# Third convolution channel split between VectorE and GpSimd, and a head's exact scores placed ahead of a later head's first scores

## The chip, the cores and the metric

The kernel runs on one core of a Trainium2 chip. The metric is the device time of one execution in microseconds (us), as the median over the timed runs. One more execution is recorded by the hardware profiler; its own time and its span (first to last instruction) are given with the profile. TensorE is called PE in the profile, VectorE DVE, ScalarE ACT, GpSimd POOL; SP issues most of the transfers.

## The reference, cut to what matters

Two layers of an encoder block on one sequence of 512 positions with 1024 features, float32. Each layer is a half-weighted gated feed-forward block, a mixing block, a second feed-forward block and a final norm. The change lies in the mixing block, which has eight attention heads and a convolution side by side:

```python
def conv_group(u_raw, conv_w, conv_b, ln_g, ln_b):
    a, g = u_raw[..., :CONV_W], u_raw[..., CONV_W:]
    u = a * jax.nn.sigmoid(g)
    y = lax.conv_general_dilated(          # causal, depthwise, 31 taps, 512 features
        u, conv_w[:, None, :].astype(u.dtype),
        window_strides=(1,), padding=[(CONV_K - 1, 0)],
        dimension_numbers=('NWC', 'WIO', 'NWC'), feature_group_count=CONV_W)
    y = y + conv_b
    return jax.nn.silu(layer_norm(y, ln_g, ln_b))

# in each layer
attn = mla_group(...)                      # 8 heads, block-causal softmax attention
conv = conv_group(p[..., o_cv:], ...)
x = x + jnp.concatenate([attn, conv], axis=-1) @ w_out[l]
```

The layer norm of the convolution needs the sum over all 512 features at each position, so it cannot begin before all of them are convolved.

## The kernel before, in words

Features lie on the 128 partitions and the 512 positions along a row, so the 512 convolved features are four tiles of 128 x 512, which the program calls channels 0 to 3. Full-precision products are made of three passes of float32r matmuls (lines 155 to 157). Between the two feed-forward blocks of a layer stands `mix_body`: projections, the queries and keys, then the heads, the convolution, the norm of the convolution and the output projection.

**Convolution** (lines 882 to 901). The string `CONV = "DAAD"` says for each channel who works. Kind D: ScalarE writes the 31st tap and the bias into the one PSUM bank named `cv` (line 886), VectorE adds the other thirty taps one by one, each a SCALAR_TENSOR_TENSOR in that bank (line 890), and ScalarE copies the bank back to SBUF (line 900). Kind A: ScalarE writes the first term to a tile `y` in SBUF, and for each of the thirty taps ScalarE makes a product `pr` (line 894, three buffers) and GpSimd adds it to `y` (line 898). Each tap of shift s works on a row of 512 - s, so the forms run from 511 down to 482 and the width tells which tap a row is. Lines 912 to 914 add the four channels on GpSimd into `ysum` (t in the rows), and line 916 is the matmul of that sum, the first step of the norm; matmuls of the output projection whose inputs are there already stand behind it on PE.

**Channels and their inputs.** `glu` (lines 616 to 624) makes the input `u` of a channel out of two projections. Channel 2 is projected just ahead of the heads, channel 3 in the middle of the first two heads.

**Heads.** `ORDER = "t0m1s3v4o5"` with `for step in range(H + 6)` writes the program's order: in each step come t (`turn`) for head `step`, m (`maxima`) for the head one behind, s (`scores`) for the head three behind, v (`values`) four behind and o (`turn_out`) five behind. `turn` transposes queries and keys on PE (line 808), ScalarE copies them out (line 811), GpSimd casts them (line 815). `maxima` makes first scores with the cast tiles in four matmuls (line 824), VectorE takes the row maxima (line 825, four reductions), transposes them (line 827, tile `mt`), and SP's queue writes them into a row of the queries by four small transfers (line 830). `scores` makes the exact scores with that row in four matmuls (line 837) and ScalarE takes the exponentials (line 840). `values` follows (line 848).

**What sets the order.** Tile's scheduler turns the program's order into one in-order queue for each engine, after a timeline of its own; a PSUM bank (seven of the name `ps`, one `cv`) is handed on when its readers are done, which makes waits of its own. So the order in which stages are written decides which bank waits for whom.

Of the kernel before, what the change touches and what calls it, by code (L numbers as in the profile page):

```python
# [7 lines left out]
FP = mybir.dt.float32  # L8
# [3 lines left out]
AF = mybir.ActivationFunctionType  # L12
ALU = mybir.AluOpType
AX = mybir.AxisListType

P = 128
D = 1024
S = 512
# [13 lines left out]
CK = 31  # L32
# [7 lines left out]
FRB = 9  # L40
RING = 40
WIDE = 5
CONV = "DAAD"
PAUSE = 16
LATE = ((), (), (), (0, 1, 2, 3), (4, 5, 6, 7))
SEQ = "q0 R c1 q1 q2 qo k kt tt uq uk c2"
# [7 lines left out]
E3 = 3  # L54
WOG = 3
WOP = 4
ORDER = "t0m1s3v4o5"
TURN = "AA"

VECS = [("g1", 8), ("gm", 8), ("g2", 8), ("gp", 8), ("gql", 3), ("gkl", 2),  # L60
# [12 lines left out]
def encoder_kernel(ctx: ExitStack, tc: tile.TileContext, xT, consts, vecs, rgain, wgu1, wd1,  # L73
# [10 lines left out]
    psum = ctx.enter_context(tc.tile_pool(name="psum", bufs=7, space=PSUM))  # L84
    uid = [0]

    def nm(s):
        uid[0] += 1
        return f"{s}{uid[0]}"
# [4 lines left out]
    def tmp(w=S, dt=FP):  # L94
        return tmps.tile([P, w], dt, tag="t", name=nm("t"))
# [7 lines left out]
    V, A, G, T = nc.vector, nc.scalar, nc.gpsimd, nc.tensor  # L103
# [100 lines left out]
    def spread(r):  # L204

        dg = tmp()
        V.tensor_tensor(dg.rearrange("p (t j) -> p t j", t=NT),
                        ident[:, None, :].to_broadcast([P, NT, P]),
                        r[:, :, None].to_broadcast([P, NT, P]), ALU.mult)
        ps = bank()  # L210
        T.matmul(ps, ones, dg, start=True, stop=True)
        return ps
# [22 lines left out]
    order = {}  # L235
# [372 lines left out]
    def mix(l, gx, norm, done):  # L608
        with tc.tile_pool(name="k", bufs=4) as kpool:
            mix_body(kpool, l, gx, norm, done)  # L610

    def mix_body(kpool, l, gx, norm, done):
        u = []
        ys = [None if kind == "D" else kpool.tile([P, S], FP, tag="y", name=nm("y"), bufs=2) for kind in CONV]

# [251 lines left out]

        STAGES = [({"t": turn, "m": maxima, "s": scores, "v": values, "o": turn_out}[c], int(d)) for c, d in zip(ORDER[::2], ORDER[1::2])]
        for step in range(H + 6):
# [11 lines left out]
        cw, cb = vv(l, "cw"), vv(l, "cb")  # L881
        for c in range(4):
            kind = CONV[c]
            acc = psum.tile([P, S], FP, tag="cv", name=nm("cv"), bufs=1) if kind == "D" else ys[c]
            tap = lambda k: cw[:, c * CK + k:c * CK + k + 1]
            A.activation(acc, u[c], AF.Identity, scale=tap(CK - 1), bias=cb[:, c:c + 1])  # L886
            for k in range(CK - 2, -1, -1):
                s = CK - 1 - k
                if kind == "D":
                    V.scalar_tensor_tensor(acc[:, s:], u[c][:, :S - s], tap(k), acc[:, s:], ALU.mult, ALU.add)  # L890
                    continue
                pr = kpool.tile([P, S], FP, tag="pr", name=nm("pr"), bufs=3)
                if kind == "A":
                    A.activation(pr[:, s:], u[c][:, :S - s], AF.Copy, scale=tap(k))  # L894
                else:
                    G.tensor_scalar(pr[:, s:], u[c][:, :S - s], tap(k), None, ALU.mult)
                with tc.issue_after(order["keys"]) if s >= PAUSE or c > 1 else nullcontext():
                    order["conv"] = G.tensor_tensor(acc[:, s:], acc[:, s:], pr[:, s:], ALU.add).ins  # L898
            if kind == "D":
                A.copy(u[c], acc)  # L900
                ys[c] = u[c]
# [24 lines left out]
        pr = spread(r)  # L926
        early_groups(range(E3, WOG))
        lg, lb = vv(l, "lg"), vv(l, "lb")
        cv = []
        for c in range(4):  # L930
            z = tmp()
            V.tensor_tensor(z, ys[c], pr, ALU.mult)
            s = tmp()
# [224 lines left out]
```

## Time and profile before

| | |
|---|---|
| median of 3 runs (lowest, highest) | 1810.32 us (1808.76, 1815.42) |
| profiled execution: its time, its span | 1808.44 us, 1806.6 us |
| mean granted TensorE clock | 0.983 |
| PE busy | 1746.0 us (97%) |
| DVE busy | 1382.6 us (77%) |
| ACT busy | 942.3 us (52%) |
| POOL busy | 289.7 us (16%) |

A row of the timeline reads: start in us from the span's start, length in us, engine, line of the program, operation, tile written<-tiles read, count, and in brackets the idle time just before with what ended it. Rows of equal instructions that follow each other are merged. A row of a window reads: the stretch, its length, then busy time and count for PE, PE's weight loads, DVE, ACT and POOL, the granted TensorE clock (1.00 is full), the share of the DMA engines and GB/s.

### The profile page before, as it was taken

What the parts mean: (1) busy time and instruction counts of PE and PEld (TensorE: products, weight loads), DVE (VectorE), ACT (ScalarE), POOL (GpSimd) and SP (SyncE); (2) the same over time, 40 slices, a digit from 0 to 9 for tenths busy, and PEclk for the clock granted to TensorE, in tenths of its full rate; (3) what the DMA queues carried; (4) which work ended last, traced back from release to release, by engine and by line L of the source; (5) the groups of instructions that cost most, each with busy time, mean ns of one, the idle gap of its engine ahead of it and who ended that gap; (6) DMA issues with size and microseconds to landing.
All of it is one profiled execution on the core that took longest, in us unless ns stands there. A gap on an engine that the chain in (4) does not pass through costs nothing.

```text
span 1806.6 us, 22073 instructions
## 1 busy us (share of the span) xinstructions
PE 1746.0 (97%) x8006; PEld 1446.8 (80%) x8006; DVE 1382.6 (77%) x2001; ACT 942.3 (52%) x1404; POOL 289.7 (16%) x268
## 2 busy tenths in 40 slices
PE   8999999999959999999999999999999699999998
PEld 7888888888748888888888888888977488888886
DVE  8967886688828877878799778865976398688784
ACT  6534444467745544445555344454767455444453
POOL 2000000057752000000000000000687420000000
PEclk9999999999979999999999999999999799999999
DMA  9454435325106344352924344343260253544345
GB/s 288 144 171 140 150 96 151 105 77 139 26 25 209 126 155 141 107 163 81 290 94 168 112 152 143 116 134 100 74 152 2 104 129 126 177 141 126 131 123 157
DMA packets 122429, 236.74 MB, mean 131 GB/s; under 512 B 11216, under 2 KB 58832, under 8 KB 122320
## 3 DMA queue, kind: packets, MB, share of 16 engines
q1 hardware_dynamic: 118000, 222.11, 38.3%
q0 software_dynamic: 3456, 12.58, 3.8%
q8 instruction: 63, 1.03, 0.2%
q10 hardware_dynamic: 864, 0.64, 0.1%
q14 instruction: 46, 0.38, 0.1%
HBM read 207.99 MB, written 25.17 MB: 129 GB/s over the span
## 4 chain that ended last, share of the span: by engine, by line
PE 81%; POOL 6%; DVE 5%; issue 3%; ACT 2%; DMA 2%; SPq 0%; POOLq 0%; ACTq 0%; DVEq 0%
PE ps L155 26%; PE ps L157 26%; PE ps L156 26%; POOL y L898 4%; DVE cv L890 1%; DVE wl L242 1%; PE ps L837 1%; PE ps L848 1%; DMA raw<-in_wgu 1%; DVE fr L339 1%; ACT pr L894 1%; PE ps L193 0%; DMA rg<-in_rgain 0%; DMA x<-in_xT 0%; PE ps L824 0%
## 5 line engine op out<-in xcount | busy, mean ns | idle before, releaser
L156 PE MATMUL ps<-wl,r 128*128 128x512 f32 (+2 forms) x1434 | 547.9, 384 | 1.4 <-DVE wl L242 1.4
L157 PE MATMUL ps<-wh,r 128*128 128x512 f32 (+2 forms) x1434 | 545.2, 384 | 0.0
L155 PE MATMUL ps<-wh,r 128*128 128x512 f32 (+2 forms) x1434 | 529.3, 384 | 2.7 <-ACT wh L240 1.7
L240 ACT CAST wh<-fr 128x1024 fp32r<-128x1024 f32 x255 | 267.0, 1050 | 241.8 <-PE ps L157 111.3
L157 PE MATMUL ps<-r,wl 128*128 128x512 f32 x944 | 367.0, 390 | 0.5 <-POOL wl L150 0.5
L156 PE MATMUL ps<-r,wh 128*128 128x512 f32 x944 | 366.9, 390 | 0.0
L155 PE MATMUL ps<-r,wh 128*128 128x512 f32 x944 | 364.0, 395 | 0.7 <-ACT wh L144 0.5
L242 DVE TENSOR_TENSOR wl<-fr,wh 128x1024 fp32r<-128x1024 f32 x255 | 309.8, 1218 | 49.4 <-ACT wh L240 48.0
L155 PEld LDWEIGHTS ps<-wh,r 128*128 128x128 f32 x1434 | 269.4, 188 | 55.1 <-ACT wh L240 2.6
L156 PEld LDWEIGHTS ps<-wl,r 128*128 128x128 f32 x1434 | 269.6, 188 | 53.7 <-DVE wl L242 1.9
L157 PEld LDWEIGHTS ps<-wh,r 128*128 128x128 f32 x1434 | 269.4, 188 | 52.5 <-DVE r L268 0.4
L144 ACT CAST wh<-raw 128x1024 fp32r<-128x1024 f32 (+2 forms) x142 | 139.8, 990 | 217.3 <-PE ps L156 91.9
L155 PEld LDWEIGHTS ps<-r,wh 128*128 128x128 f32 x944 | 177.8, 189 | 40.6 <-ACT r L161 1.1
L156 PEld LDWEIGHTS ps<-r,wh 128*128 128x128 f32 x944 | 177.9, 188 | 38.7 <-issue 2.0
L157 PEld LDWEIGHTS ps<-r,wl 128*128 128x128 f32 x944 | 177.8, 188 | 38.7 <-POOL wl L150 1.3
L150 DVE TENSOR_TENSOR wl<-raw,wh 128x1024 fp32r<-128x1024 f32 (+3 forms) x126 | 145.8, 1159 | 76.2 <-ACT wh L144 75.4
L898 POOL TENSOR_TENSOR y<-y,pr 128x509 f32<-128x509 f32 (+15 forms) x120 | 158.2, 1319 | 48.8 <-ACT pr L894 42.7
L339 DVE TENSOR_TENSOR fr<-fr,fr 128x1024 f32<-128x1024 f32 x112 | 136.3, 1217 | 11.0 <-DMA fr<-in_wgu 11.0
L487 DVE TENSOR_TENSOR x<-ps,x 128x512 f32<-128x512 f32 x120 | 81.6, 686 | 53.8 <-PE ps L157 53.4
L369 ACT ACTIVATE e<-e,rtok 128x256 f32<-128x256 f32 x120 | 60.0, 508 | 71.6 <-DVE e L360 70.9
L894 ACT ACTIVATE pr<-r,vec 128x511 f32<-128x511 f32 (+14 forms) x120 | 82.9, 713 | 21.5 <-POOL y L898 21.5
L890 DVE SCALAR_TENSOR_TENSOR cv<-r,vec,cv 128x511 f32<-128x511 f32 (+14 forms) x120 | 88.0, 733 | 5.9 <-ACT cv L886 3.8
(199 smaller groups left out, 1630.8 us busy)
## 6 DMA issues: line engine op xcount, KB each, us to landing
fr<-in_wgu SPq DMA_DIRECT2D x175, 512.0 KB
raw<-in_wd SPq DMA_DIRECT2D x56, 512.0 KB
d<-e SPq DMA_DIRECT2D x176, 128.0 KB
r<-d SPq DMA_DIRECT2D x88, 256.0 KB
raw<-in_wd SPq DMA_DIRECT2D x32, 384.0 KB
raw<-in_wcv SPq DMA_DIRECT2D x16, 512.0 KB
raw<-in_wout SPq DMA_DIRECT2D x16, 512.0 KB
raw<-in_wgu SPq DMA_DIRECT2D x8, 512.0 KB
```

Of the source, the lines that this page charges most:

```text
L144: A.copy(hi[:, :w], raw[:, :w])
L150: (G if kind in POOLW.split() else V).tensor_tensor(lo[:, :w], raw[:, :w], hi[:, :w].bitcast(FP), ALU.subtract)
L155: T.matmul(o, lh, rh, start=first, stop=False, skip_group_check=free)
L156: T.matmul(o, lh, rl, start=False, stop=False, skip_group_check=free)
L157: T.matmul(o, ll, rh, start=False, stop=last, skip_group_check=free)
L240: order["cast"] = A.copy(hi[:, :w], src[:, :w]).ins
L242: V.tensor_tensor(lo[:, :w], src[:, :w], hi[:, :w].bitcast(FP), ALU.subtract)
L339: V.tensor_tensor(oh, ah, bh, ALU.add)
L487: V.tensor_tensor(xm, pd.rearrange("p (a t j) -> p t a j", a=4, t=NT), xm, ALU.add)
L890: V.scalar_tensor_tensor(acc[:, s:], u[c][:, :S - s], tap(k), acc[:, s:], ALU.mult, ALU.add)
L894: A.activation(pr[:, s:], u[c][:, :S - s], AF.Copy, scale=tap(k))
L898: order["conv"] = G.tensor_tensor(acc[:, s:], acc[:, s:], pr[:, s:], ALU.add).ins
```

## The change

Channel 2 becomes a new kind, M: ScalarE writes the first term into the `cv` bank, VectorE adds the taps of shift 1 to 12 there, ScalarE copies the bank to `y`, and the taps of shift 13 to 30 stay as they were (product by ScalarE, addition by GpSimd). GpSimd's own products, which no channel used, go. In the heads' order, s3 now stands ahead of m1: in each step the exact scores of the head three behind come ahead of the first scores of the head one behind. Behind `mix_body`'s norm every engine has the order it had; both layers change alike. The lines of the program behind line 43 move by one.

```diff
--- before.py
+++ after.py
@@ -40,7 +40,8 @@
 FRB = 9
 RING = 40
 WIDE = 5
-CONV = "DAAD"
+CONV = "DAMD"
+MIXED = 12
 PAUSE = 16
 LATE = ((), (), (), (0, 1, 2, 3), (4, 5, 6, 7))
 SEQ = "q0 R c1 q1 q2 qo k kt tt uq uk c2"
@@ -54,7 +55,7 @@
 E3 = 3
 WOG = 3
 WOP = 4
-ORDER = "t0m1s3v4o5"
+ORDER = "t0s3m1v4o5"
 TURN = "AA"
 
 VECS = [("g1", 8), ("gm", 8), ("g2", 8), ("gp", 8), ("gql", 3), ("gkl", 2),
@@ -881,21 +882,21 @@
         cw, cb = vv(l, "cw"), vv(l, "cb")
         for c in range(4):
             kind = CONV[c]
-            acc = psum.tile([P, S], FP, tag="cv", name=nm("cv"), bufs=1) if kind == "D" else ys[c]
+            split_at = {"D": CK, "M": MIXED + 1, "A": 0}[kind]
+            acc = psum.tile([P, S], FP, tag="cv", name=nm("cv"), bufs=1) if split_at else ys[c]
             tap = lambda k: cw[:, c * CK + k:c * CK + k + 1]
             A.activation(acc, u[c], AF.Identity, scale=tap(CK - 1), bias=cb[:, c:c + 1])
             for k in range(CK - 2, -1, -1):
                 s = CK - 1 - k
-                if kind == "D":
+                if s < split_at:
                     V.scalar_tensor_tensor(acc[:, s:], u[c][:, :S - s], tap(k), acc[:, s:], ALU.mult, ALU.add)
                     continue
+                if s == split_at:
+                    A.copy(ys[c], acc)
                 pr = kpool.tile([P, S], FP, tag="pr", name=nm("pr"), bufs=3)
-                if kind == "A":
-                    A.activation(pr[:, s:], u[c][:, :S - s], AF.Copy, scale=tap(k))
-                else:
-                    G.tensor_scalar(pr[:, s:], u[c][:, :S - s], tap(k), None, ALU.mult)
+                A.activation(pr[:, s:], u[c][:, :S - s], AF.Copy, scale=tap(k))
                 with tc.issue_after(order["keys"]) if s >= PAUSE or c > 1 else nullcontext():
-                    order["conv"] = G.tensor_tensor(acc[:, s:], acc[:, s:], pr[:, s:], ALU.add).ins
+                    order["conv"] = G.tensor_tensor(ys[c][:, s:], ys[c][:, s:], pr[:, s:], ALU.add).ins
             if kind == "D":
                 A.copy(u[c], acc)
                 ys[c] = u[c]
```

The order that this gives, at the three places that matter (layer 0; r678_3684 is channel 2's input, r706_3808 channel 3's, y510_2859 channel 2's sum; numbers of tiles are the program's).

VectorE, from channel 2's input on; ps696 to ps698 are the first scores of head 0, mt699 its maxima, t704 and t705 belong to channel 3's input. Before:

```order
L623 SCALAR_TENSOR_TENSOR r678_3684<-ps672_3648,t677_3682 128x512
L825 TENSOR_REDUCE mx_104<-ps696_3755 128x1
L825 TENSOR_REDUCE mx_104<-ps697_3756 128x1
L825 TENSOR_REDUCE mx_104<-ps698_3757 128x1
L825 TENSOR_REDUCE mx_104<-ps696_3755 128x1
L827 STREAM_TRANSPOSE mt699_3766<-mx_104 128x128
L618 TENSOR_TENSOR t704_3803<-ps700_3772,R546_2998 128x512
L621 SCALAR_TENSOR_TENSOR t705_3806<-ps692_3724,R546_2998 128x512
L825 TENSOR_REDUCE mx_104<-ps713_3828 128x1
```

And now, from the first of the same reductions on; the seven taps of widths 511 to 505 of channel 2 stand right ahead of these rows, behind the instruction that makes r678_3684:

```order
L826 TENSOR_REDUCE mx_104<-ps696_3755 128x1
L826 TENSOR_REDUCE mx_104<-ps697_3756 128x1
L826 TENSOR_REDUCE mx_104<-ps698_3757 128x1
L892 SCALAR_TENSOR_TENSOR cv894_4445<-r678_3684,vec_80,cv894_4445 128x504
L892 SCALAR_TENSOR_TENSOR cv894_4445<-r678_3684,vec_80,cv894_4445 128x503
L892 SCALAR_TENSOR_TENSOR cv894_4445<-r678_3684,vec_80,cv894_4445 128x502
L892 SCALAR_TENSOR_TENSOR cv894_4445<-r678_3684,vec_80,cv894_4445 128x501
L892 SCALAR_TENSOR_TENSOR cv894_4445<-r678_3684,vec_80,cv894_4445 128x500
L826 TENSOR_REDUCE mx_104<-ps696_3755 128x1
L619 TENSOR_TENSOR t704_3803<-ps700_3772,R546_2998 128x512
L622 SCALAR_TENSOR_TENSOR t705_3806<-ps692_3724,R546_2998 128x512
L828 STREAM_TRANSPOSE mt699_3766<-mx_104 128x128
```

Seven taps have come ahead of head 0's first three reductions and five ahead of the fourth, and the transpose that ends head 0's maxima stands behind two instructions of channel 3's input.

PE, at the fourth step of the heads; r681 and r684 are head 0's queries and keys, r709 and r712 the cast ones of head 2, ps733 and ps736 the transposes of head 4. Before:

```order
L808 MATMUL ps720_3854<-cst_79,kn519_2872 101x128 x4
L824 MATMUL ps723_3863<-r712_3826,r709_3817 128x128
L824 MATMUL ps724_3864<-r712_3826,r709_3817 128x384
L824 MATMUL ps725_3865<-r712_3826,r709_3817 128x512
L837 MATMUL ps727_3880<-r681_3693,r684_3702 128x512
L837 MATMUL ps728_3881<-r681_3693,r684_3702 128x384
L837 MATMUL ps728_3881<-r681_3693,r684_3702 128x128
L837 MATMUL ps729_3882<-r681_3693,r684_3702 128x256
L808 MATMUL ps733_3893<-cst_79,q518_2871 101x128 x4
L824 MATMUL ps723_3863<-r712_3826,r709_3817 128x256
```

And now:

```order
L809 MATMUL ps720_3854<-cst_79,kn519_2872 101x128 x4
L838 MATMUL ps723_3863<-r681_3693,r684_3702 128x512
L838 MATMUL ps724_3864<-r681_3693,r684_3702 128x384
L838 MATMUL ps724_3864<-r681_3693,r684_3702 128x128
L838 MATMUL ps725_3865<-r681_3693,r684_3702 128x256
L825 MATMUL ps729_3876<-r712_3826,r709_3817 128x128
L825 MATMUL ps730_3877<-r712_3826,r709_3817 128x384
L825 MATMUL ps731_3878<-r712_3826,r709_3817 128x512
L809 MATMUL ps733_3893<-cst_79,q518_2871 101x128 x4
L809 MATMUL ps736_3902<-cst_79,kn519_2872 101x128 x4
L838 MATMUL ps739_3911<-r687_3711,r690_3720 128x512
L838 MATMUL ps740_3912<-r687_3711,r690_3720 128x384
```

The four exact scores of head 0 have come ahead of the three first scores of head 2, and the exact scores of head 1 (r687) ahead of head 2's fourth.

ScalarE, at the exponentials of head 5; ps814 to ps816 hold its exact scores before, ps810 to ps812 now. Before:

```order
L840 ACTIVATE r817_4176<-ps814_4169 128x512
L840 ACTIVATE r818_4177<-ps815_4170 128x512
L894 ACTIVATE pr902_4470<-r678_3684,vec_80 128x503
L840 ACTIVATE r819_4178<-ps816_4171 128x256
L894 ACTIVATE pr903_4473<-r678_3684,vec_80 128x502
L894 ACTIVATE pr904_4476<-r678_3684,vec_80 128x501
L161 CAST r824_4202<-ps823_4197 128x512
```

And now:

```order
L901 COPY r706_3808<-cv913_4514 128x512
L841 ACTIVATE r813_4159<-ps810_4152 128x512
L841 ACTIVATE r814_4160<-ps811_4153 128x512
L897 ACTIVATE pr901_4478<-r678_3684,vec_80 128x493
L841 ACTIVATE r815_4161<-ps812_4154 128x256
L897 ACTIVATE pr902_4481<-r678_3684,vec_80 128x492
L897 ACTIVATE pr903_4484<-r678_3684,vec_80 128x491
L162 CAST r824_4202<-ps823_4197 128x512
```

Between the second and the third exponential of head 5 stands one product of channel 2 in both; before it is the tap of width 503, now the tap of width 493.

## The prediction

> **What bounds the kernel now.** I read the page's slices first, then the chain of waits, then the timelines of PE, GpSimd and ScalarE around the two dips.
>
> ```profile
> PE   8999999999959999999999999999999699999998
> POOL 2000000057752000000000000000687420000000
> PE 81%; POOL 6%; DVE 5%; issue 3%; ACT 2%; DMA 2%; SPq 0%; POOLq 0%; ACTq 0%; DVEq 0%
> ```
>
> PE is busy nearly everywhere, except in one slice of each layer, right where GpSimd's work ends; GpSimd holds 6% of the chain though it is busy 16% of the span. The timelines (PE, then GpSimd, then ScalarE) show the place:
>
> ```profile
> 504.20 0.63 PE L865 MATMUL ps<-cst,t 128*128 128x128 f32 x4 [0.82 <-DVE t L855]
> 522.81 2.07 PE L916 MATMUL ps<-t,onesm 128*128 128x512 f32 x2 [17.98 <-POOL t L914]
> ...
> 1416.57 2.08 PE L916 MATMUL ps<-t,onesm 128*128 128x512 f32 x2 [17.96 <-POOL t L914]
> ...
> 490.22 10.61 POOL L898 TENSOR_TENSOR y<-y,pr 128x503 f32<-128x503 f32 x8 [0.76 <-ACT pr L894]
> 500.78 1.28 POOL L912 TENSOR_TENSOR t<-r,y 128x512 f32<-128x512 f32 x1
> 502.00 18.07 POOL L898 TENSOR_TENSOR y<-y,pr 128x495 f32<-128x495 f32 x14
> 520.15 1.26 POOL L913 TENSOR_TENSOR t<-t,y 128x512 f32<-128x512 f32 x1
> 521.49 1.26 POOL L914 TENSOR_TENSOR t<-t,r 128x512 f32<-128x512 f32 x1
> ...
> 488.88 0.60 ACT L840 ACTIVATE r<-ps 128x512 f32<-128x512 f32 x1 [0.27 <-PE ps L837]
> 489.37 0.70 ACT L894 ACTIVATE pr<-r,vec 128x503 f32<-128x503 f32 x1
> ```
>
> The heads end on PE at 504.83 (504.20 + 0.63), and it then stands idle for 17.98 us, in the other layer for 17.96, until GpSimd has added up channel 2 and the four channels. GpSimd works without a pause from 490.22 to 522.75: 22 additions of channel 2 and three of L912 to L914, 25 in 32.53 us, 1.30 us each. What started that run is the product of width 503, which ScalarE makes in the slot behind head 5's second exponential (489.37).
>
> **GpSimd's side.** In the new order that same slot, behind head 5's second exponential, makes the product of width 493 instead of 503, because twelve taps have left the queue. Behind it GpSimd has 12 additions (493 to 482) and the three sums: 15 x 1.30 = 19.5 us instead of 32.5. If head 5 comes when it came, the last sum ends 13.0 us earlier. Head 5 comes later by some d, and the gain of a layer is 13.0 - d as long as GpSimd, and not the heads, is last: the heads would end at 504.8 + d, the sums at 509.75 + d, so GpSimd stays last. All of the question is d. Products and additions saved ahead of the slot cost and bring nothing: GpSimd waits there for ScalarE anyway (the 0.76 us in the row of 490.22).
>
> **VectorE's side: what d is made of.**
>
> ```profile
> 438.76 0.69 DVE L623 SCALAR_TENSOR_TENSOR r<-ps,t 128x512 f32<-128x512 f32 x1
> 440.43 0.81 ACT L886 ACTIVATE y<-r,vec 128x512 f32<-128x512 f32 x1
> 442.91 1.38 DVE L825 TENSOR_REDUCE mx<-ps 128x1 fp32r<-128x128 f32 x3 [3.45 <-PE ps L824]
> 447.81 0.42 DVE L825 TENSOR_REDUCE mx<-ps 128x1 fp32r<-128x256 f32 x1 [3.52 <-PE ps L824]
> 448.27 0.31 DVE L827 STREAM_TRANSPOSE mt<-mx 128x128 f32<-128x128 f32 x1
> 449.59 0.68 DVE L621 SCALAR_TENSOR_TENSOR t<-ps,R 128x512 f32<-128x512 f32 x1
> 453.73 5.48 DVE L890 SCALAR_TENSOR_TENSOR cv<-r,vec,cv 128x511 f32<-128x511 f32 x7 [1.05 <-ACT cv L886]
> 464.98 0.30 DVE L827 STREAM_TRANSPOSE mt<-mx 128x128 f32<-128x128 f32 x1
> ```
>
> Channel 2's first term is ready at 441.24, and seven taps take 5.48 us (0.78 each): until 446.7. Head 0's first three reductions follow at 446.7 to 448.1, five taps take 3.9 to 452.0, the fourth reduction 0.4, the two steps of channel 3's input 0.6 each, the transpose 0.3: head 0's maxima end at 453.9 instead of 448.58, 5.3 late. The cover was VectorE's idle time: 1.7 of the first wait (441.24 to 442.91) and the 3.52 of the second hide 5.2 of the 9.4 us of taps and the 1.2 us of the two steps. Head 1's four reductions (1.6) and the last step of channel 3's input (0.6) follow, then ScalarE's first term (0.8): channel 3's taps, which began at 453.73, begin at 456.9, or some tenths earlier since neighbours in these rows overlap by 0.08 each. I take 456.6, 2.9 late.
>
> What PE does meanwhile:
>
> ```profile
> 448.67 2.30 SPq L830 DMA_DIRECT2D r<-mt  x4
> 488.18 1.43 DMA r<-mt
> 455.57 1.33 PE L824 MATMUL ps<-r,r 101*128 101x128 f32 x3 [3.91 <-POOL r L815]
> 456.70 4.47 PE L837 MATMUL ps<-r,r 101*128 101x512 f32 x8
> 469.61 2.32 PE L837 MATMUL ps<-r,r 101*128 101x512 f32 x8
> 456.70:461.00 4.30, 4.30 (x10) 2.44 (x9) 4.19 (x8) 1.24 (x3) 3.61 (x4) 0.50 0.15 28
> ```
>
> Head 0's row of maxima needs 2.30 us of issue on SP and 1.43 for the last transfer: there at 457.6. Before, PE waited 3.91 us for GpSimd's cast of head 2 and made head 2's first scores, then head 0's exact ones at 456.70. Now the exact ones stand first, and queued behind them are head 2's first scores, the transposes of head 4 and head 1's exact scores; all wait until 457.6. So the reordering does not fill the hole of 3.91 us, as it would with the row there by 452: the hole ends at 457.6 instead of 455.57, 2.0 later, and head 0's exact scores themselves come 0.9 later.
>
> Head 2 costs the rest. Its maxima ended 11.55 us behind channel 3's first tap (465.28 - 453.73); the same thirteen taps and the same reductions stand ahead of them now, so they end at 453.73 + 2.9 + 11.55 = 468.2, and with 3.7 us of transfers head 2's exact scores start at 471.9, not 469.61: d = 2.3. Before, the row was there by 469.0 and nobody waited; the exact scores of one more head (2.3 us of PE, the row of 469.61) lay between, and the new order takes them out of that distance. From head 2's to head 5's exact scores PE has the same number of stages as before, so d stays at 2.3 if no later row is late.
>
> So the gain is 13.0 - 2.3 = 10.7 us a layer; two layers 21.4. Channel 3's own chain ends 2.9 later too, long before its sum is wanted. ScalarE's copy of the `cv` bank (0.6) lies in its idle time; it makes twelve products fewer. GpSimd's other rows are unchanged. The matmul of the sum (L916) then starts at 512.1, behind an idle of 512.1 - 507.1 = 5.0 us, and all behind it keeps its order and moves as a block, weight transfers included: they wait for buffers that the norm's last steps release.
>
> Two prices have no row. The transfers of head 0's maxima now follow weight transfers issued at 451, of which the nearest row tells the time to landing:
>
> ```profile
> 451.10 0.89 POOL L148 DMA_DIRECT2D wl<-in_wout  x1 [1.88 <-ACT wl L147]
> wl<-in_wout POOLq DMA_DIRECT2D x8, 512.0 KB, 7.6
> ```
>
> From 0, where they pass beside it, to 458.7 + 1.43 = 460.1, 2.5 late, where they wait for it; I take 0, since they are tiny. And whether VectorE keeps its old pace from head 3 on: from d back to 0.9 (PE comes late, so VectorE catches up) to one more such loss of 2.3 us, d = 4.6.
>
> **The clock.** The window 456.70 to 461.00 shows a granted clock of 0.50 behind the idle of 3.91 us, and the next one shows the same behind the 17.98:
>
> ```profile
> 522.80:527.00 4.20, 4.19 (x9) 2.68 (x10) 2.08 (x4) 1.55 (x4) 0.00 (x0) 0.54 0.00 0
> ```
>
> Behind 5.0 us of idle I take the same loss as now, so it leaves the sum as it is. The Trainium skill (TensorE: Matmul & The Clock Gate, "What's actually happening") says that the clock halves after an idle window of about 3.4 us, and that these windows run freely. The rows of 3.91 and 17.98 us agree; by that rule an idle of 5.0 us may or may not hold a whole window, so that the sum would be this one or the warm case below.
>
> **A shared port.** GpSimd's additions ran beside back-to-back taps at 1.26 us each, below their mean of 1.30:
>
> ```profile
> 456.68 3.79 POOL L898 TENSOR_TENSOR y<-y,pr 128x487 f32<-128x487 f32 x3
> ```
>
> I charge nothing for it. The Trainium skill (SBUF — State Buffer, "Who interferes with whom") holds that a VectorE instruction with two SBUF inputs blocks GpSimd's reads for its whole length; a tap has one such input beside the bank, and its column of weights as a second if that counts. If it did, twelve taps would stop GpSimd for up to 9.4 us a layer; the row above speaks against it.
>
> **The sum.** 1808.44 - 2 x 10.7 = 1787.0 us for a profiled execution. The median of the runs stood 1.9 above that execution, within the runs' own spread of 6.7; I add half of it and forecast 1788.
>
> **The rivals.**
> - *Later heads lose time as well* (VectorE stays the last in heads 3 to 5): d of 4.6 to 8, gain of 8.4 to 5 a layer, 1793 to 1800. For it: VectorE was busy 9.86 and 9.96 of 10 us between 460 and 480 (third number in the windows below), and gets 12 taps more. Against: the taps of channel 3 are the same 30, and the extra ones are done by 452.
> - *The heads keep their time, or the clock stays up*: d near 0.9, or the nine matmuls behind the gap at full clock, which saves 0.46 of their 4.19 us, 1.9. Gain 12 to 14 a layer, 1780 to 1784. For it: VectorE has idle time from 484 on (3.77 busy of 7). Against: head 2's row is late by the sum above.
> - *Slower: the row of maxima becomes the bound.* In every step PE waits at the exact scores, since the new order has taken 2.3 us out of the way from maxima to scores, and behind the waiting matmul stands everything else. The gain is gone when d reaches 13.0, which is 2.1 us for each of the six heads 2 to 7 on top of the 0.9; with 2.7 us each d is 17, and the kernel takes 1816. For it: head 2 already waits 2.3. Against: head 2 has thirteen taps ahead of its maxima's end, later heads five or six.
> - *It does not do what it says*: GpSimd's additions wait for products, not the reverse, so that fewer additions bring little. Against: ScalarE waited for GpSimd in nearly every product behind 503, as in the row of 509.81 below, and at the one product that waits for PE's last transposes (504.87) it loses 0.87. Time 1803 to 1812.
>
> ```profile
> 460.00:470.00 10.00, 9.45 (x57) 7.79 (x57) 9.86 (x20) 7.01 (x13) 5.65 (x7) 0.91 0.00 0
> 470.00:480.00 10.00, 10.00 (x70) 8.57 (x69) 9.96 (x23) 6.41 (x13) 5.61 (x7) 1.00 0.01 3
> 484.00:491.00 7.00, 7.00 (x52) 6.13 (x50) 3.77 (x10) 5.20 (x11) 6.00 (x6) 1.00 0.00 0
> ...
> 509.81 0.70 ACT L894 ACTIVATE pr<-r,vec 128x487 f32<-128x487 f32 x1 [0.60 <-POOL y L898]
> 504.87 0.59 ACT L161 CAST r<-ps 128x512 fp32r<-128x512 f32 x1 [0.87 <-PE ps L865]
> ```
>
> **How the numbers follow.** The forecast (d from 0.9 to 4.6; 1783 to 1793) gets 0.60, later heads losing 0.17, the better case 0.13, slower 0.04, no effect 0.06. The range, with both outer cases taken in down to two in ten left out: 1778 to 1798. About 0.5% (9 us) is what a measurement of this kernel can tell from no change. Faster by more than that: 0.60 + 0.17 + 0.13 = 0.90; within it 0.06; slower 0.04.
>
> **What would show it.** Right: PE's idle before the matmul of the sum falls from 17.98 to about 5 us in both layers, still put down to GpSimd; additions of 1.30 us run without a pause from the product of width 493 on, which begins near 491.7; the transposes of head 0's and head 2's maxima end at 453.9 and 468.2; the last transposes of the heads near 507. Wrong: idle of PE before exact scores in several heads, additions longer than 1.35 us, or pauses of GpSimd behind 493.

## The result, and the profile after

The changed kernel takes 1792.49 us (median of 4 runs, 1789.96 to 1793.53) against 1810.22 us (4 runs, 1808.76 to 1815.42): a ratio of 0.9895, 95% interval 0.9873 to 0.9917. That is faster, by 17.7 us where 22 were forecast, and inside the range. The profiled execution has a span of 1788.2 us against 1806.6, 18.4 us less where the sum said 21.4.

The page of the changed kernel, its slices of PE and GpSimd, and its chain of waits by engine:

```profile
PE   8999999999889999999999999999999899999998
POOL 2000000058642000000000000000676410000000
PE 84%; DVE 5%; POOL 4%; DMA 3%; issue 2%; ACT 1%; SPq 1%; POOLq 0%; DVEq 0%; ACTq 0%
```

The slices that stood at 5 and 6 for PE are now 8, and GpSimd's share of the chain fell from 6% to 4%. The two gaps, in the timeline of PE (the heads' last transposes, then the matmul of the sum, for each layer):

```profile
506.89 0.63 PE L866 MATMUL ps<-cst,t 128*128 128x128 f32 x4 [0.82 <-DVE t L856]
511.93 2.08 PE L917 MATMUL ps<-t,onesm 128*128 128x512 f32 x2 [4.41 <-POOL t L915]
...
1390.66 0.63 PE L866 MATMUL ps<-cst,t 128*128 128x128 f32 x4 [0.83 <-DVE t L856]
1397.46 2.08 PE L917 MATMUL ps<-t,onesm 128*128 128x512 f32 x2 [6.17 <-POOL t L915]
```

PE waits 4.41 and 6.17 us where it waited 17.98 and 17.96. How GpSimd's last stretch begins, in its timeline, in layer 0 and then in layer 1, and behind it the two products of ScalarE, one for each layer, that set its length:

```profile
492.33 5.16 POOL L899 TENSOR_TENSOR y<-y,pr 128x493 f32<-128x493 f32 x4 [2.75 <-ACT pr L897]
497.80 5.12 POOL L899 TENSOR_TENSOR y<-y,pr 128x489 f32<-128x489 f32 x4 [0.32 <-ACT pr L897]
...
1376.81 10.37 POOL L899 TENSOR_TENSOR y<-y,pr 128x494 f32<-128x494 f32 x8 [3.13 <-ACT pr L897]
...
491.49 0.70 ACT L897 ACTIVATE pr<-r,vec 128x493 f32<-128x493 f32 x1
1375.95 1.90 ACT L897 ACTIVATE pr<-r,vec 128x494 f32<-128x494 f32 x3
```

In layer 0 the run starts with width 493 and has 12 additions and three sums, 19.5 us from 492.33 to 511.87, as predicted, but for one pause of 0.32 us (second row) where none was expected. In layer 1 it starts with width 494: 13 additions. The sentence ahead of the prediction, that both layers change alike, does not hold: in layer 1 ScalarE's queue holds one product fewer ahead of head 5's exponentials. Before, both layers had width 503 there.

VectorE and PE at the heads' start, in their timelines (end of head 0's maxima, channel 3's first taps, end of head 2's maxima; head 0's and head 2's exact scores; the last two rows are head 0 in layer 1):

```profile
453.38 0.30 DVE L828 STREAM_TRANSPOSE mt<-mx 128x128 f32<-128x128 f32 x1
456.91 6.26 DVE L892 SCALAR_TENSOR_TENSOR cv<-r,vec,cv 128x511 f32<-128x511 f32 x8 [0.63 <-ACT cv L888]
468.17 0.30 DVE L828 STREAM_TRANSPOSE mt<-mx 128x128 f32<-128x128 f32 x1
458.32 4.51 PE L838 MATMUL ps<-r,r 101*128 101x512 f32 x8 [2.56 <-DMA r<-mt]
471.77 2.40 PE L838 MATMUL ps<-r,r 101*128 101x512 f32 x8 [1.55 <-DMA r<-mt]
...
1337.16 0.30 DVE L828 STREAM_TRANSPOSE mt<-mx 128x128 f32<-128x128 f32 x1
1343.14 4.13 PE L838 MATMUL ps<-r,r 101*128 101x512 f32 x8 [3.60 <-DVE cv L892]
```

To compare layers and kernels, the table below counts from the start of head 0's first scores (442.54 and 1336.27 before, 442.74 and 1326.53 after) to the end of the heads' last transposes, and to the start of the matmul of the sum. Each pair is layer 0 / layer 1 of the profiled execution; the numbers are differences of rows like the ones above.

| kernel | median, us | ratio to before, 95% interval | heads end | matmul of the sum |
|---|---|---|---|---|
| before | 1810.2 | | 62.3 / 62.3 | 80.3 / 80.3 |
| the change | 1792.5 | 0.9895 (0.9873, 0.9917) | 64.8 / 64.8 | 69.2 / 70.9 |
| order alone | 1818.9 | 1.0035 (1.0020, 1.0050) | 61.4 / 67.2 | 82.8 / 88.6 |
| split alone | 1784.9 | 0.9848 (0.9824, 0.9872) | 69.1 / 72.5 | 69.0 / 72.3 |
| split alone, six taps | 1795.6 | 0.9921 (0.9906, 0.9936) | 62.3 / 69.8 | 72.2 / 74.6 |
| twelve taps left out | 1777.6 | 0.9808 (0.9781, 0.9834) | 62.3 / 66.2 | 64.4 / 66.0 |
| left out, new order | 1788.7 | 0.9867 (0.9843, 0.9891) | 61.0 / 66.2 | 66.7 / 71.8 |
| change, one transfer left out | 1788.8 | 0.9884 (0.9870, 0.9900) | 64.7 / 66.4 | 68.5 / 70.2 |
| change, PE kept busy in the gap | 1792.3 | 0.9896 (0.9881, 0.9911) | 66.9 / 64.6 | 71.3 / 70.8 |
| before, PE kept busy in the gap | 1807.6 | 0.9983 (0.9970, 0.9996) | 65.5 / 62.3 | 83.6 / 80.3 |
| change, sums on VectorE | 1787.1 | 0.9867 (0.9851, 0.9884) | 67.0 / 69.3 | 69.7 / 69.2 |
| split, taps late | 1779.9 | 0.9832 (0.9815, 0.9848) | 62.3 / 62.5 | 64.8 / 65.0 |
| split, taps late, sums on VectorE | 1777.2 | 0.9813 (0.9799, 0.9828) | 62.3 / 62.5 | 64.3 / 64.5 |
| the same, sums first | 1774.5 | 0.9807 (0.9791, 0.9824) | 62.3 / 62.3 | 63.6 / 63.6 |

The change's 18.4 us are thus 11.1 of layer 0 and 9.4 of layer 1 up to the matmul of the sum, less 1.1 lost between the two layers, 0.7 behind the second (not by the clock, and left open), and 0.2 ahead of the first. Of the 1.1, 0.7 is the clock: by the trace's clock records, half clock lasts 5.3 us from the matmul of the sum on in layer 0, where it lasted 3.9, and half of that difference is lost. The 30 us from that matmul on in layer 0, in the windows of before and then of the change (granted clock is the number behind the count):

```profile
522.81:552.81 30.00, 29.63 (x120) 0.94 0.44 167
```

```profile
511.93:541.93 30.00, 29.62 (x117) 0.91 0.42 159
```

### The profile page after: what moved, and what is told of

Same layout as the page of the kernel before. It is cut to its first block, busy times and chain, and to the rows that moved or that the text cites. A ratio compares the mean times of both kernels' runs of the same rounds, so it can differ in the third digit from the quotient of the medians.

```text
span 1788.2 us, 22027 instructions
## 1 busy us (share of the span) xinstructions
PE 1748.7 (98%) x8006; PEld 1447.6 (81%) x8006; DVE 1399.5 (78%) x2025; ACT 926.7 (52%) x1382; POOL 260.4 (15%) x244
## 4 chain that ended last, share of the span: by engine, by line
PE 84%; DVE 5%; POOL 4%; DMA 3%; issue 2%; ACT 1%; SPq 1%; POOLq 0%; DVEq 0%; ACTq 0%
PE ps L156 27%; PE ps L158 27%; PE ps L157 27%; POOL y L899 3%; DVE cv L892 2%; PE ps L838 1%; PE ps L849 1%; DMA d<-e 1%; DMA raw<-in_wgu 1%; DMA fr<-in_wgu 1%; DMA r<-d 1%; DVE wl L243 1%; DVE mx L826 1%; PE ps L194 0%; PE ps L809 0%
## 5 line engine op out<-in xcount | busy, mean ns | idle before, releaser
L899 POOL TENSOR_TENSOR y<-y,pr 128x497 f32<-128x497 f32 (+15 forms) x96 | 127.9, 1333 | 51.2 <-ACT pr L897 46.9
L892 DVE SCALAR_TENSOR_TENSOR cv<-r,vec,cv 128x511 f32<-128x511 f32 (+9 forms) x144 | 105.7, 734 | 9.3 <-ACT cv L888 6.5
L399 DVE TENSOR_TENSOR r<-r,r 128x512 fp32r<-128x512 f32 x88 | 58.1, 678 | 44.6 <-ACT r L398 44.4
```

Source lines behind the costliest of these rows:

```text
L899: order["conv"] = G.tensor_tensor(ys[c][:, s:], ys[c][:, s:], pr[:, s:], ALU.add).ins
```

## The experiments

### The two halves of the change apart

The theory behind the prediction, called Q below, says that a layer's gap is set by what is left in GpSimd's queue behind head 5's second exponential. It leaves open what each of the two edits does to that queue. First the order alone:

```diff
-ORDER = "t0m1s3v4o5"
+ORDER = "t0s3m1v4o5"      (CONV as before)
```

> The new order of the heads alone, channel 2 as before. Theory Q (a layer's gap is set by GpSimd's queue behind head 5's second exponential: additions still to come there, plus three sums, 1.30 us each): in the written order ScalarE now has the product of width 506 in that slot instead of 503, so 25 + 3 steps instead of 22 + 3, 3.9 us more; the heads themselves come perhaps 1.5 us earlier, since no taps stand ahead of head 0's maxima and its exact scores fill the hole of 3.91 us. Matmul of the sum 2.4 us later, 1813 us (1809 to 1817). Rival H (only the heads' own time counts): 1800 to 1806. Rival N (the order is neutral): 1810.

Measured: 1818.9 us, ratio 1.0035, some 6 us slower. How GpSimd's last stretch begins in layer 0, in its timeline:

```profile
489.47 10.59 POOL L898 TENSOR_TENSOR y<-y,pr 128x506 f32<-128x506 f32 x8 [2.29 <-ACT pr L894]
```

The stretch begins with width 506: 25 additions down to width 482 instead of 22. The heads end 0.9 us earlier in layer 0 (61.4; some 1.5 had been expected), and the matmul of the sum starts 2.5 us later (82.8; expected 2.4). In layer 1 the heads ended 4.9 us later than before (67.2), which is why the expected 1813 was too low: PE waited there for two rows of maxima (2.92 and 1.87 us), and the clock fell a second time. The rival that only the heads count falls: in layer 0 the heads were earlier and the gap longer.

Then the split alone, with the old order:

```diff
-CONV = "DAAD"
+CONV = "DAMD"             (MIXED = 12, ORDER as before)
```

> The split of channel 2 alone, heads in the old order. Theory Q: the old order lets ScalarE make more products ahead of head 5's second exponential: the next one behind it is of width 487 (layer 0) or 485 (layer 1), so 6 or 4 additions and three sums, at most 12 us, are left and GpSimd ends before the heads. PE's idle before the matmul of the sum nearly goes (under 2 us), the heads end 1.6 us late, the clock stays up: gain of some 16 to 18 us a layer, 1774 us (1768 to 1780). Rival N (the order is neutral, the twelve taps make the whole gain): 1790 to 1794, as the change. Rival H (the twelve taps delay the heads, and the new order mends a part): 1795 or more.

Measured: 1784.9 us, so the split alone is better than the change by some 7.6 us, but 11 worse than expected. The timelines of GpSimd (its last sum) and PE (last transposes, matmul of the sum):

```profile
507.16 1.27 POOL L915 TENSOR_TENSOR t<-t,r 128x512 f32<-128x512 f32 x1
509.81 0.63 PE L866 MATMUL ps<-cst,t 128*128 128x128 f32 x4 [0.83 <-DVE t L856]
510.27 1.02 PE L917 MATMUL ps<-t,onesm 128*128 128x512 f32 x2
```

The gap is gone and the clock stays up, as expected: GpSimd ends before the heads. What failed is the 1.6 us for the heads. They ended 6.8 us late in layer 0 and 10.1 in layer 1. Longer waits early in the heads and the clock behind them account for it. Two of these waits in PE's timeline of layer 0

```profile
457.38 1.33 PE L825 MATMUL ps<-r,r 101*128 101x128 f32 x3 [3.04 <-POOL r L816]
467.80 0.70 PE L838 MATMUL ps<-r,r 101*128 101x256 f32 x2 [1.53 <-DVE mx L826]
```

and the windows behind them:

```profile
470.00:474.00 4.00, 4.00 (x20) 0.50 0.01 2
474.00:478.00 4.00, 4.00 (x15) 0.71 0.02 5
```

Behind the wait of 1.53 us the granted clock falls a second time, for 6.83 us by the trace's clock records (layer 1: 10.24 us), which takes about half of that from PE, 3.4 and 5.1 us. The rest is close to what PE's waits in the heads have grown by: in sum 7.25 us where they were 4.46 (layer 1: 9.47 and 4.22), 2.8 and 5.3 us more.

So the matmul of the sum comes no earlier than in the change: at 69.0 and 72.3, where the change has 69.2 and 70.9, in sum 1.2 us later. What the split alone gains over the change in the profiled executions (6.0 us) lies elsewhere: 2.7 us behind the first of these matmuls and 3.0 behind the second, and 1.4 ahead of the first heads, where both kernels have the same instructions. Behind the matmul of the sum it keeps full clock, where the change had 0.91 and 0.94 in the same 30 us, which is 2.6 and 1.9 us:

```profile
510.27:540.27 30.00, 29.62 (x131) 1.00 0.48 178
```

### What the twelve taps cost, and what the order costs without them

```diff
                 s = CK - 1 - k
+                if c == 2 and s <= 12:
+                    continue
```

This leaves the taps of shift 1 to 12 of channel 2 out of the computation, in the kernel before and then also with the new order.

> The kernel before, with taps 1 to 12 of channel 2 left out of the computation altogether: GpSimd's relief without VectorE's load. Theory Q: head 5's slot holds width 491 (layer 0) or 488 (layer 1), 10 or 7 additions and three sums, 16.9 or 13.0 us: GpSimd ends 2.3 us behind the heads' end in layer 0 and before it in layer 1; heads on time; 1774 us (1770 to 1778). Against the split alone it shows what the taps on VectorE cost: 1.6 us a layer less what stands in GpSimd's way. Rival P (GpSimd's additions wait for products and not the reverse): above 1795.

> The same with taps 1 to 12 of channel 2 left out, and the new order of the heads. Theory Q: head 5's slot holds width 494 in both layers, 13 additions and three sums, 20.8 us, and the heads come some 1.5 us earlier: gain 13.2 a layer less the slow clock behind a gap, 1783 us (1779 to 1788), so the order costs about 9 us against the run without it. Rival N (order neutral): equal to the run without it within 3 us.

Measured: 1777.6 us with the old order, inside the expected range, and 1788.7 with the new one, 11 us worse, just above its range (the heads of layer 1 lost 4 us as with the old order). In layer 0 GpSimd ends 2.1 us behind the heads, as expected (2.3):

```profile
506.26 2.07 PE L918 MATMUL ps<-t,onesm 128*128 128x512 f32 x2 [2.09 <-POOL t L916]
```

Layer 1 of the old order was not as expected: its heads ended 3.9 us late (66.2) though VectorE had no taps to add there, behind a wait of PE for maxima and a second stretch of half clock of 6.83 us by the clock records:

```profile
1343.57 1.57 PE L837 MATMUL ps<-r,r 101*128 101x384 f32 x6 [2.23 <-DVE mx L825]
```

So the new order costs 11 us without the taps and 7.6 with them, and the taps in their place on VectorE cost 7.3 us in the old order (1784.9 against 1777.6) and 3.8 in the new one (1792.5 against 1788.7); the run that the 7.3 is counted from has that loss in it. All that speaks for the rival that additions wait for products are single pauses of 0.2 to 0.5 us inside GpSimd's last stretches.

### How many taps are free

```diff
-MIXED = 12
+MIXED = 6                 (split alone, old order)
```

> The split alone, heads in the old order, with six taps on VectorE instead of twelve. Theory D (the taps delay the heads only as far as they exceed VectorE's idle time ahead of head 0's maxima, 5.2 us, and six take 4.7): the heads end on time, within 0.5 us of the kernel before; head 5's slot holds width 497 in layer 0 (16 additions and three sums, 24.7 us, gain 7.8) and 493 in layer 1 (12 and three, 19.5 us, gain 13.0): 1787.5 us (1784 to 1791). Rival (any tap there delays the heads, by the 0.4 us a tap that twelve cost with it): heads 2.4 us late, 1792 or more.

Measured: 1795.6 us, above the range, though layer 0 does what Theory D says:

```profile
505.53 0.63 PE L866 MATMUL ps<-cst,t 128*128 128x128 f32 x4 [0.83 <-DVE t L856]
516.10 2.08 PE L917 MATMUL ps<-t,onesm 128*128 128x512 f32 x2 [9.94 <-POOL t L915]
```

The heads end at 62.3, exactly on time, and the gap is 9.94 us. In layer 1 head 0's maxima are also on time (6.04 behind the first scores, as before), yet the heads end 7.5 us late: a wait of 1.89 us for VectorE comes ahead of exact scores at 1365.12, and a second stretch of half clock (10.24 us) follows. That six taps are free is shown for layer 0; for layer 1 neither side is, since the second stretch alone takes about 5 us. In layer 0 a delay of 0.4 us a tap is not there.

### The row of maxima

The prediction took 0, out of 0 to 2.5 us, for what weight transfers do to the row of head 0's maxima. From the end of the maxima (453.68 and 1337.46) to the exact scores (458.32 and 1343.14) it took 4.64 us in layer 0 and 5.68 in layer 1, where 2.30 + 1.43 = 3.73 had been expected. To test the cause, one transfer was left out:

```diff
-            G.dma_start(out=lo[:, :w], in_=src, accum_op=ALU.add)
+            if two is not None:       (None for the fourth of the weights)
+                G.dma_start(out=lo[:, :w], in_=src, accum_op=ALU.add)
```

> The change with one transfer left out: the last accumulating weight transfer of GpSimd's queue ahead of the heads' exact scores (512 KB, issued at 451.3), so that one weight's low part is wrong. Theory T (head 0's row of maxima is late because its four tiny transfers share the engines with the weights): head 0's exact scores start 3.4 to 3.8 us behind the end of its maxima in both layers, not 4.6 to 6.6 as in the four traces with the transfer, and the heads end at 506.9 (d of 2.7) or earlier in every layer; 1788 us (1785 to 1790) where those layers that waited longest gain 1 to 2. Rival (the row's time is its own, whatever else moves): 4.6 us or more, 1792.

Measured: 1788.8 us, as expected by Theory T. The time alone does not decide it, since the interval of its ratio (0.9870 to 0.9900) overlaps the change's; the row does. The windows of the change, then of this kernel (the share of the DMA engines is the number behind the clock):

```profile
450.00:454.00 4.00, 1.55 (x5) 0.80 0.99 208
454.00:458.00 4.00, 1.77 (x9) 0.50 0.75 141
```

```profile
450.00:454.00 4.00, 1.26 (x7) 0.95 0.74 199
454.00:458.00 4.00, 2.57 (x8) 0.50 0.02 6
```

The end of head 0's maxima and its exact scores in this kernel's timeline:

```profile
453.13 0.30 DVE L829 STREAM_TRANSPOSE mt<-mx 128x128 f32<-128x128 f32 x1
456.96 4.61 PE L839 MATMUL ps<-r,r 101*128 101x512 f32 x8 [1.43 <-DMA r<-mt]
```

With the engines idle (0.02 instead of 0.75) the row takes 3.53 us, and 3.36 in layer 1. The heads still end at 64.7 in layer 0: there head 2's row decides, which VectorE sets, as the prediction said. In layer 1 they end at 66.4, later than the change's and against the expectation, with a second stretch of half clock of 3.41 us by the clock records. Part of the 3.7 us is another order of ScalarE's products: leaving the transfer out moved them, too, and GpSimd's last stretch begins with width 493 in both layers.

One row with nothing left out agrees. In layer 1 of the run with the sums on VectorE (below), which has another order, the DMA engines had a share of 0.11 between the end of head 0's maxima and the exact scores, and the row took 3.37 us:

```profile
1337.86 0.31 DVE L828 STREAM_TRANSPOSE mt<-mx 128x128 f32<-128x128 f32 x1
1341.54 2.68 PE L838 MATMUL ps<-r,r 101*128 101x512 f32 x3 [0.30 <-DMA r<-mt]
```

In the other new-order rows, where that share was 0.50 to 0.84, it took 4.1 to 6.6 us. How long within that did not follow the share.

### The clock behind the gap

```diff
+        with tc.issue_after(order["last"]):      (the last of the heads' transposes)
+            idle(9)                              (18 rows of 128 x 128 on PE)
         pm = bank()
```

> The change, with nine idle 128 x 128 matmuls into an unused bank on PE between the heads' last transposes and the matmul of the sum; every other order is the change's, and the time of the gap's end stays GpSimd's. Theory C (half the clock behind the gap costs on its own: in the change the rows from 511.93 to 517.2 ran at half clock, 5.3 us in each layer, of which 2.6 us are lost): PE has work in the gap, the granted clock stays at 1.00 behind it, gain of 2 to 2.6 us a layer, 1787 to 1789 us in the same company. Rival (the loss behind the gap is the norm's own chain of waits): 1792, no difference.

Measured: 1792.3 us, no difference. It is inconclusive. PE was busy for 2.17 of the gap's microseconds only, idle for 2.39 more, and the clock fell all the same:

```profile
459.47 4.61 PE L838 MATMUL ps<-r,r 101*128 101x512 f32 x8 [4.39 <-DVE cv L892]
508.75 2.17 PE L120 MATMUL ps<-ones 128*128 128x128 f32 x18
513.31 1.99 PE L919 MATMUL ps<-t,onesm 128*128 128x512 f32 x2 [2.39 <-POOL t L915]
```

Its first row shows another thing: instruction for instruction this is the change up to the gap, and head 0's row took 6.47 us instead of 4.64, and the heads ended 2.1 us later (66.9 against 64.8); half clock at the heads' start also lasted longer, 13.65 us by the clock records instead of 10.24. So the test was made again where the heads don't wait for that row, on the kernel before, with 70 instead of 9:

> The kernel before, with seventy idle 128 x 128 matmuls into an unused bank on PE in the gap of 18 us (some 17 us at 0.12 us a row, as measured for eighteen rows in the change), all else as before. Theory C: the granted clock behind the gap is 1.00, so the matmul of the sum and the eight behind it run in 2.3 instead of 4.2 us: 1.9 us a layer, 1806.5 us. Rival (the half clock behind the gap is hidden by the norm's waits): 1810.

Measured: 1807.6 us, ratio 0.9983 (0.9970 to 0.9996): 2.6 us between the medians, of 3.8 expected, with an interval that ends close to 1. The rows of both layers:

```profile
528.43 1.12 PE L918 MATMUL ps<-t,onesm 128*128 128x512 f32 x2 [2.41 <-POOL t L914]
1421.20 2.08 PE L918 MATMUL ps<-t,onesm 128*128 128x512 f32 x2 [2.41 <-POOL t L914]
```

The same idle of 2.41 us left full clock in layer 0 (1.12 us for the matmul of the sum) and half clock in layer 1 (2.08 us). The price of the half clock is on the path; whether it is paid behind a short gap differs between two passes of the same program.

### The sums, and the taps moved

```diff
-        G.tensor_tensor(ysum, ys[0], ys[1], ALU.add)
-        G.tensor_tensor(ysum, ysum, ys[2], ALU.add)
+        V.tensor_tensor(ysum, ys[0], ys[1], ALU.add)
+        V.tensor_tensor(ysum, ysum, ys[2], ALU.add)     (and YP = 0: the third one, too)
```

> The change, with the three additions of the four channels on VectorE instead of GpSimd (0.69 instead of 1.27 us each, and the first one out of GpSimd's queue). Theory Q: in layer 0 head 5's slot holds width 493 as in the change, and the end of the sums comes 2.4 us earlier; in layer 1 the written order happens to put width 490 there instead of 494, four additions fewer, and GpSimd ends before the heads: the gap of 6.17 us goes altogether. Gain 2.4 + 6 us, and 2 to 2.6 us more in each layer where the clock stays up: 1780 us (1777 to 1785). Rival (GpSimd's tail is hidden by ScalarE's products): 1790 to 1793.

Measured: 1787.1 us, above the range. The tail did what Theory Q says (matmul of the sum 2.7 us behind the heads in layer 0, none in layer 1), but the heads ended later than the change's, at 67.0 and 69.3: head 0's row took 6.59 us in layer 0, and in layer 1, whose order is another one, VectorE was late. What the tail gained the heads lost in part.

The next kernel keeps the old order, and moves VectorE's part of channel 2 behind channel 3, where VectorE was idle in part (busy for 3.77 of the 7 us from 484 on in the kernel before):

```diff
-CONV = "DAMD"
+CONV = "DALD"
+            if kind == "L":           (y starts with the tap of shift 13, zeros ahead of it; GpSimd adds 14 to 30)
+        for c in range(4):
+            if CONV[c] == "L":        (behind channel 3)
+                acc = cvbank()
+                first(acc, c)
+                taps(acc, c, range(1, MIXED + 1))
+                V.tensor_tensor(ys[c], ys[c], acc, ALU.add)
```

> The heads in the old order, and the same split of channel 2 with VectorE's part moved behind channel 3: GpSimd starts channel 2 with the tap of shift 13, VectorE makes the first term and the taps of shift 1 to 12 in the bank when channel 3 has left it (about 489), between the last heads' reductions, and adds the bank to GpSimd's sum. Theory Q with the cost of the taps in VectorE's place ahead of head 0's maxima: the heads keep their time (last transposes at 504 in layer 0), GpSimd has nine additions and one sum behind head 5's slot, then VectorE's addition and two sums: 506.5, 1.7 us behind the heads. 1776 us (1771 to 1781), like the run with the taps left out. Rival (VectorE's load as such delays the heads, wherever it stands): 1785, like the split alone.

> The same, with the last two sums on VectorE: they end at 505.3, 0.5 us behind the heads' last transposes, so PE does not wait long enough to lose its clock. 1769 us (1765 to 1775); if the tail were not on the path: as without it, 1776.

Measured: 1779.9 and 1777.2 us. The heads end at 62.3 to 62.5 in all four layers, so the twelve taps cost the heads at most 0.2 us there: it is their place that costs, not VectorE's load. Against the run with the taps left out the first one is 2.3 us slower; in the profiled executions that is not in the heads (the matmul of the sum at 64.8 and 65.0, in that run 64.4 and 66.0). Behind the second matmul 2.4 us are lost: PE has waited 2.56 us there for GpSimd's sums, with 6.83 us of half clock by the records, where that run had no gap. The first time is inside its range, the second 2 us above its own. In the second one the matmul of the sum waited 2.00 us, not 0.5, since the last sum stood behind the subtraction of the last transposes in VectorE's queue; the last kernel puts the sums ahead of it:

```diff
+        with tc.issue_after(total):              (the last sum)
+            at.append(split(order["out"]))       (the last transposes)
         pm = bank()
```

> The late split with two sums on VectorE, and the sums ahead of the last heads' subtraction in VectorE's queue (there, the last sum stood behind it and waited for the last transposes, so the matmul of the sum came 2.0 us behind the heads). Theory Q: GpSimd's last addition ends at 502.8, VectorE's addition and the two sums at 505.5, so the matmul of the sum follows the heads within 0.7 us: 1.5 us a layer less, and up to 0.9 us where the clock stays up: 1773 us (1771 to 1776). Rival (the sums are not the last wait): 1777.

Measured: 1774.5 us (1773.0 to 1778.8), ratio 0.9807, inside the range. The timelines of VectorE and PE:

```profile
502.51 0.68 DVE L926 TENSOR_TENSOR y<-y,cv 128x512 f32<-128x512 f32 x1
503.22 0.69 DVE L938 TENSOR_TENSOR t<-t,y 128x512 f32<-128x512 f32 x1
503.95 0.69 DVE L939 TENSOR_TENSOR t<-t,r 128x512 f32<-128x512 f32 x1
502.74 0.63 PE L866 MATMUL ps<-cst,t 128*128 128x128 f32 x4 [0.82 <-DVE t L856]
504.69 2.08 PE L943 MATMUL ps<-t,onesm 128*128 128x512 f32 x2 [1.32 <-DVE t L939]
```

VectorE's addition stands behind the last quotient (L856), so the sums end 1.3 us behind the heads, where 0.7 had been expected, and PE's matmul runs at half clock even behind 1.32 us. This kernel beats both: 18 us under the change, 36 under the kernel before.

## Why the prediction was right, and where it was off

**GpSimd's queue.** Right. The gap fell because fewer additions are left behind head 5's slot, at 1.29 us each (5.16 for four), and GpSimd stayed the last. The one pause of 0.32 us in layer 0 is a small form of what the prediction listed as a sign of being wrong; the 15 steps took 1.28 us each instead of 1.30, and that this makes up for the pause is luck. With the order alone (width 506), the taps left out (491 and 494 in layer 0) and six taps (497) the gap went with the width in that slot.

**The sum was made for one layer and doubled.** This is the step that failed: "two layers 21.4". Layer 0 gave 11.1 (10.7 predicted); layer 1 gave 9.4, because its slot holds width 494: one addition of 1.3 us more, and 0.4 in sum for a product that starts 0.7 us later, behind channel 3's copy and the third exponential, less the pause of layer 0. The order of both layers could be read before; the equal layers of the kernel before (17.98 and 17.96) suggested that one was enough. Of the 3.0 us by which the sum was too high this is 1.3, and layer 0 gives back 0.4. The other 2.0 stand against "moves as a block": they were lost outside the two stretches that the sum looked at, 1.8 of them behind the matmuls of the sum, and 0.7 of these are the clock.

**d, the heads' delay.** Right in size: 2.5 and 2.4 us, where 2.3 stood. Its steps hold: head 0's maxima end at 453.68 (predicted 453.9), channel 3's taps start at 456.91 (456.6), head 2's maxima end at 468.47 (468.2), head 2's exact scores start at 471.77 (471.9). Later heads lose nothing more.

**The price taken as 0** was mis-sized: head 0's row took 0.9 and 2.0 us longer than the sum said, by contention with weights, as the run without the transfer and the row with a share of 0.11 show. In this profile it stays hidden behind head 2's row. Where it reaches 6.5 us, as in two other traces of the same order, d becomes 4.6 to 4.7, the row's 1.9 us and the longer half clock together: the rival "later heads lose as well" in effect, by another place. Whether this is why the median stands 2.5 us above the profiled execution was not shown.

**The clock** was charged as before. In layer 0 it cost 0.7 us more: half clock until 517.2, 5.3 us behind the matmul of the sum, against 3.9 before, though the gap is shorter. In layer 1 nothing more (0.94 against 0.93 before). The Trainium skill (TensorE: Matmul & The Clock Gate, "What's actually happening") calls the windows free-running, which fits two layers of one program that differ, and puts the fall behind an idle window of about 3.4 us; the rows of 1.32 and 2.41 us above had half clock behind less, and the count in the last section shows that a window need not be idle throughout.

**The shared port** plays no part: GpSimd's additions beside the twelve taps took what they took before, 1.25 us at 444.40 and 2.87 for the two from 446.56 (before, without taps there: 1.25 at 444.19 and 2.87 for the two from 446.36).

**What the prediction did not ask**: what each edit does alone. The order costs 6 us by itself and some 8 in the change. ScalarE then makes fewer products ahead of head 5, so GpSimd is the last again. By itself that is 2.5 us in layer 0, and in layer 1 the heads lose 4.9 us as well. In the change the earlier heads (64.8 against 69.1 and 72.5) make up for the gap, and most of what it costs is the half clock behind the gap. Read from its queue, the split alone would have been forecast as the better kernel.

## What to carry to other kernels

Where an engine works down a queue behind a slot of another one, the order of that other engine decides how much is left; read it for every layer and for each edit alone, since a scheduler shifts it with edits elsewhere. Work that is to relieve one engine costs nothing on the next only where that one is idle and nobody waits behind it: the same twelve taps cost 7 us ahead of the first maxima and 2 behind channel 3, both counted from a run without them that itself lost 3.9 us in one layer's heads. A gap that an edit leaves on PE has a second price behind it, the half clock. And an edit that puts a wait for a small transfer first in a queue exposes that queue to whatever else is being moved.

## What the runs showed of the hardware that was not expected

The granted clock changes, by the trace's clock records, in stretches that are multiples of 3.41 us (from 3.41 to 27.31 in these traces), and in some layers it falls a second time in the heads, behind a wait of 1.5 to 2.4 us. The kernel before with its gap filled is the same as the kernel before up to the gap; the windows of both, before first:

```profile
462.00:466.00 4.00, 3.45 (x18) 1.00 0.00 0
466.00:470.00 4.00, 4.00 (x34) 1.00 0.01 1
```

```profile
466.00:470.00 4.00, 3.23 (x17) 0.82 0.00 0
470.00:474.00 4.00, 4.00 (x21) 0.50 0.00 0
474.00:478.00 4.00, 4.00 (x19) 0.83 0.02 5
```

and PE's row ahead of the fall in the second one:

```profile
466.77 1.57 PE L837 MATMUL ps<-r,r 101*128 101x384 f32 x6 [1.61 <-DVE mx L825]
```

In the second trace PE waited 1.61 us for VectorE, where it had waited 0.55, the clock fell for 6.83 us, and the heads ended 3.2 us later. Elsewhere an idle of 1.61 us at the same matmul (the late split, layer 0) left the clock up. The kept traces show in part what decides. In each trace all changes of the clock lie on a grid of 3.41 us, and the 14 traces together have 7144 windows of that grid at full clock. Counted by the share of a window in which PE was busy (by the profile's modelled ends of matmuls), and by what the next window's clock was:

| PE busy in a window at full clock | windows | followed by half clock |
|---|---|---|
| below 46% | 66 | 66 |
| 46 to 68% | 42 | 17 |
| above 68% | 7036 | 0 |

So the share of a whole window counts, and not the length of one idle, and the cases above fit. The idle of 1.61 us that cost the clock lay in a window with 53% busy, that of the late split in one with 66%. The two equal gaps of 2.41 us left 46% in layer 0, where the clock stayed, and 39% in layer 1, where it fell. The 1.32 us of the last kernel shared its window with the 0.82 ahead of the heads' last transposes: 37%. This was read from the traces afterwards and not tested by a run; what decides between 46 and 68%, and how long half clock then lasts, stays open. The clock moves single layers by 3 to 5 us and is behind several of the missed times above.
